# Both late passages with norm, rotation and splits in fixed lanes, key stacks by DMA, and weights rounded by ScalarE outside attention

## The chip, the cores and the metric

The kernel runs on one core of a Trainium2 chip. The core has a matrix engine (TensorE, PE in the profile), three elementwise engines (VectorE is DVE, ScalarE is ACT, GpSimd is POOL) and a queue engine (SyncE, SP) that issues all DMAs of this kernel. Each engine works off its own instructions strictly in order and waits on semaphores for the others. The metric is the time of one execution in microseconds, as the device measures it.

## The reference, cut to what matters

A block of two transformer layers works on 512 latent tokens and, in the first layer, on 256 context tokens, with 1024 channels. Both layers have the same frame:

```python
u_lat = modulate(x_lat, ng[0], ml[0], ml[1])          # rms_norm * g * (1+scale) + shift
...
x_lat = x_lat + ml[2] * rms_norm(y_lat, ng[1])
h_lat = swiglu(modulate(x_lat, ng[2], ml[3], ml[4]), ffn_w_in[l], ffn_w_out[l])
x_lat = x_lat + ml[5] * rms_norm(h_lat, ng[3])
```

The mixer of layer 0 is a gated linear recurrence, that of layer 1 is windowed attention with a sink, 16 query heads on 4 key heads of 64 channels, rotated by position:

```python
q, k, v = jnp.split(u @ w_qkv, [C_Q, C_Q + C_KV], axis=-1)
q = apply_rope(split_heads(q, C_HEADS), cos, sin)
k = apply_rope(split_heads(k, C_KV_HEADS), cos, sin)
k_c, v_c = jnp.split(u_c @ w_qkv[:, C_Q:], 2, axis=-1)
```

So between the FFN of layer 0 and the attention, and again between the attention's output product and the FFN of layer 1, stands the same **passage**: a norm of y over the channels, the residual sum x, a norm of x, and the modulated u, of which the next matrix products are made.

## The kernel before, in words

**Tiles.** Activations lie with channels on the 128 partitions: eight tiles of 128 x 512 for the latents, one for each 128 channels. The latents go through the passages in two halves of 256 tokens, `HS[0]` and `HS[1]`, so that the products of one half can run beside the passage of the other.

**Split products.** Every product is made of three matmuls: an operand is rounded to a high part ("hi", `whi`, `uh`), the rest is the low part ("lo", `wlo`, `ul`), and hi x hi, lo x hi and hi x lo are added in PSUM (`gemm`, L180, and L190 to L192 with the operands swapped). A weight tile of 128 x 1024 floats comes by DMA as `raw` (512 KB, four buffers), hi is made of it by ScalarE (L132, and L154 for weights that are held over) or by GpSimd (L130), lo by VectorE (L133, L155) or GpSimd. Which engine takes the next weight is a pattern per phase, set by `engines(ph)` at L540: 'a' or 'p' for hi, 'd' or 'p' for lo. In before, hi is GpSimd's in all phases that the table doesn't name (the late recurrent phases, the layer-0 output phases, attention), and in every second weight of 'wo'.

**A passage.** `Acc.add` squares a tile on ScalarE (L348, L352) and sums the squares into two accumulators, one kept by VectorE and one by GpSimd (both L353). `rstd_bc` sums over the channels with matmuls against ones (L369), takes the root (L371, ScalarE) and the reciprocal (L373, VectorE), and spreads it over the partitions by matmuls into PSUM (L376); its product `ps_tr` is called bc here. `residual` (L435) then makes x of each tile: in a tile marked 'd', VectorE multiplies y by bc (L451) and adds it, scaled, to x (L454); in a tile marked 'p', VectorE multiplies (L447) and GpSimd adds (L449). `norm_mod` (L393) makes `nt` (L417, VectorE), `uh` (L424, ScalarE) and `ul` (L408, VectorE) of each tile.

**The two late passages.** Passage 1 (`lat_next`, L1311) stands between `po`, the FFN output of layer 0, and the attention's products of keys and values (`kv_ctx`, `kv_lat`) and queries (`q_lat`). Passage 2 (`lat_next2`) stands between `wo`, the attention's output product, and `ffn_in` of layer 1. The generators of a passage and of a product are interleaved by `merge(main, side, ratio)`. Keys are rotated by `roped` (`rx`, `ry`, L1354 to L1358) and stored by `k_stack` twice over the partitions, hi and lo (`KC` for the context, `KL` for the latents): for each key head two copies on ScalarE (L1346, L1347) and two subtractions on VectorE (L1348, L1349), each of 64 partitions.

**Order.** A scheduler with a timeline of its own orders each engine's instructions over the whole program; the kernel is built three times with other buffer slots, and the build whose own simulated time is least is taken. `follow(key, ins)` fixes that instructions with the same key stand on their engine in the order in which they are written ("a lane"). In before, each residual and each norm has a key of its own, for VectorE alone, so the two halves of a passage are free against each other.

## Time and profile before

The profiled execution took 1795.28 us; its span, from the first to the last instruction, is 1793.5 us, so 1.8 us lie around the span. The median of the runs shown is 1795.77 us (1793.75 to 1797.13).

| engine | busy us | share of the span |
|---|---|---|
| PE | 1723.8 | 96% |
| DVE | 1048.4 | 58% |
| ACT | 773.5 | 43% |
| POOL | 386.0 | 22% |

The mean granted clock of PE is 0.981. In the strip of 40 slices (each 44.8 us), the digit is the busy share in tenths:

```profile
PE   7989999999899999999999999799999899999997
DVE  3767644565767636797643536688755853322336
ACT  3965464244645545532222223434756643222311
POOL 1123403343320015200000002424443300000015
PEclk9989999999999999999999999899999999999999
```

PE is full but for the head, the slice from 448 us, those about 1125 to 1215 us (passage 1), about 1390 us (passage 2), and the end. Rows of the timeline read: start, duration, engine, line, operation, out<-in, shape, and in brackets how long the engine was idle before it and what released it.

### The profile page before, as it was taken

The numbers are of one execution on the slowest core, as the hardware profiler recorded it, in microseconds if no ns is written. First come the engines' busy times: TensorE is split into PE (matmuls) and PEld (weight loads), VectorE is DVE, ScalarE is ACT, GpSimd is POOL, SyncE is SP. The second block draws the span as 40 slices with busy tenths as digits, with TensorE's granted clock in tenths as the row PEclk, the third lists the DMA queues.
The fourth block names the chain that finished last, engine by engine and source line by source line (L and its number), as shares of the span: only waits on it lengthen the run. The fifth ranks groups of instructions, "written<-read, shape, count | busy, mean of one in ns | idle before, by whom it ended". The sixth has DMA issues, their size and how long they took to land. (4 is left out here: it accounts for less than half of the span.)

```text
span 1793.5 us, 27238 instructions
## 1 busy us (share of the span) xinstructions
PE 1723.8 (96%) x10711; PEld 1477.9 (82%) x10711; DVE 1048.4 (58%) x1723; ACT 773.5 (43%) x1342; POOL 386.0 (22%) x421
## 2 busy tenths in 40 slices
PE   7989999999899999999999999799999899999997
PEld 3978678798899989988888888787787898888886
DVE  3767644565767636797643536688755853322336
ACT  3965464244645545532222223434756643222311
POOL 1123403343320015200000002424443300000015
PEclk9989999999999999999999999899999999999999
DMA  8546656211345554767545324312021443233323
GB/s 307 162 130 201 205 171 215 69 48 48 92 121 148 170 156 136 240 211 227 174 147 167 119 74 126 95 40 68 2 60 36 130 130 94 83 99 113 94 66 115
DMA packets 83696, 228.18 MB, mean 127 GB/s; under 512 B 9296, under 2 KB 14160, under 8 KB 83568
## 3 DMA queue, kind: packets, MB, share of 16 engines
q1 hardware_dynamic: 83568, 226.45, 41.1%
q8 instruction: 84, 1.38, 0.3%
q14 instruction: 44, 0.36, 0.1%
HBM read 224.31 MB, written 2.10 MB: 126 GB/s over the span
## 5 line engine op out<-in xcount | busy, mean ns | idle before, releaser
L133 DVE TENSOR_TENSOR wlo<-raw,whi 128x1024 fp32r<-128x1024 f32 (+3 forms) x302 | 365.6, 1213 | 298.2 <-ACT whi L132 235.5
L132 ACT CAST whi<-raw 128x1024 fp32r<-128x1024 f32 (+2 forms) x232 | 235.2, 1015 | 478.9 <-issue 176.1
L180 PE MATMUL ps_mm<-uh,whi 128*128 128x256 f32 (+1 forms) x840 | 289.9, 345 | 3.1 <-ACT whi L132 2.9
L180 PE MATMUL ps_mm<-ul,whi 128*128 128x256 f32 (+1 forms) x840 | 287.2, 342 | 0.0
L180 PE MATMUL ps_mm<-uh,wlo 128*128 128x512 f32 (+1 forms) x840 | 286.9, 342 | 0.0
L180 PE MATMUL ps_kv<-uh,whi 128*128 128x512 f32 (+1 forms) x696 | 246.5, 354 | 0.0
L180 PE MATMUL ps_kv<-uh,wlo 128*128 128x512 f32 (+1 forms) x696 | 245.3, 352 | 0.4 <-DVE wlo L133 0.4
L180 PE MATMUL ps_kv<-ul,whi 128*128 128x512 f32 (+1 forms) x696 | 245.4, 353 | 0.0
L130 POOL TENSOR_SCALAR whi<-raw 128x1024 fp32r<-128x1024 f32 (+1 forms) x80 | 79.1, 991 | 727.1 <-PE ps_mm L180 349.3
L180 PEld LDWEIGHTS ps_mm<-uh,whi 128*128 128x128 f32 x840 | 161.8, 193 | 25.1 <-ACT whi L132 3.4
L180 PEld LDWEIGHTS ps_mm<-ul,whi 128*128 128x128 f32 x840 | 161.6, 192 | 17.9 <-issue 1.4
L180 PEld LDWEIGHTS ps_mm<-uh,wlo 128*128 128x128 f32 x840 | 161.4, 192 | 18.1 <-issue 0.6
L180 PEld LDWEIGHTS ps_kv<-uh,whi 128*128 128x128 f32 x696 | 131.8, 189 | 22.4 <-issue 2.7
L353 POOL TENSOR_TENSOR acc<-acc,sq 128x256 f32<-128x256 f32 (+1 forms) x79 | 92.6, 1174 | 261.2 <-ACT sq L352 260.2
L180 PEld LDWEIGHTS ps_kv<-uh,wlo 128*128 128x128 f32 x696 | 131.6, 189 | 18.7 <-DVE wlo L133 0.6
L180 PEld LDWEIGHTS ps_kv<-ul,whi 128*128 128x128 f32 x696 | 131.8, 189 | 17.6
L190 PE MATMUL ps_mm<-whi,uh 128*128 128x256 f32 x344 | 101.5, 296 | 9.2 <-ACT gate L793 9.2
L290 DVE SCALAR_TENSOR_TENSOR aacc<-ar,s,aacc 128x512 f32<-128x512 f32 x112 | 81.7, 755 | 35.3 <-DMA ar<-in_ada_dram 34.5
L180 PE MATMUL ps_kv<-hh,whi 128*128 128x512 f32 (+1 forms) x282 | 100.2, 355 | 0.0
L180 PE MATMUL ps_kv<-hh,wlo 128*128 128x512 f32 (+1 forms) x282 | 100.1, 355 | 0.0
L180 PE MATMUL ps_kv<-hl,whi 128*128 128x512 f32 (+1 forms) x282 | 100.0, 355 | 0.0
L191 PE MATMUL ps_mm<-wlo,uh 128*128 128x256 f32 x344 | 99.2, 290 | 0.0
(325 smaller groups left out, 3493.8 us busy)
## 6 DMA issues: line engine op xcount, KB each, us to landing
raw<-in_ff_in_dram SPq DMA_DIRECT2D x138, 512.0 KB, 3.6
ar<-in_ada_dram SPq DMA_DIRECT2D x192, 256.0 KB, 4.2
raw<-in_ff_out_dram SPq DMA_DIRECT2D x52, 512.0 KB, 3.6
raw<-in_rec_a_dram SPq DMA_DIRECT2D x34, 512.0 KB, 4.3
raw<-in_rec_v_dram SPq DMA_DIRECT2D x16, 512.0 KB, 3.6
raw<-in_rec_g_dram SPq DMA_DIRECT2D x16, 512.0 KB, 4.3
raw<-in_rec_o_dram SPq DMA_DIRECT2D x16, 512.0 KB, 4.0
...
```

What stands on the lines that cost most here:

```text
L130: nc.gpsimd.tensor_scalar(hi[:, :n], raw[:, :n], 1.0, 0.0, ALU.mult, ALU.add)
L132: nc.scalar.copy(hi[:, :n], raw[:, :n])
L133: (nc.gpsimd if cfg["lo"][q % len(cfg["lo"])] == "p" else nc.vector).tensor_sub(lo[:, :n], raw[:, :n], hi[:, :n].bitcast(F32))
L180: mm(ps_, a, b, start=(i == 0), stop=(i == len(q) - 1))
L190: mm(ps, ah, hi[:, s], start=(k == 0), stop=False)
L191: mm(ps, ah, lo[:, s], start=False, stop=False)
L290: nc.vector.scalar_tensor_tensor(a, raw, s_, a, ALU.mult, ALU.add)
L353: (nc.vector if i else nc.gpsimd).tensor_add(d, d, q)
```

## The change

Six edits go together:

1. `engines`: hi by ScalarE in every phase but attention, where it stays with GpSimd; lo by VectorE everywhere.
2. Both passages: all tiles of all halves 'd' (VectorE multiplies and adds), one lane key for residual and norm, "next" for both halves of passage 1, "next2a" and "next2b" for the halves of passage 2; `uh` on ScalarE stands in the lane too. With `own=2` the squares of the last two tiles are not added to an accumulator but summed over directly by more matmuls against ones.
3. The last tile of an output product that runs in halves (`po`, and `pf` of layer 1) keeps its square apart in the same way.
4. `k_stack`: one cast (`kth`, ScalarE) and one subtraction (`ktl`, VectorE, in lane "next") on all 128 partitions, and then eight DMAs from SBUF to SBUF of 64 partitions by SP for each of the six calls. The context's keys are read from PSUM, without the copy `kc`.
5. `q_lat` for the first two query tiles runs by halves: the half `HS[0]` inside passage 1, beside the passage of the other half, and `HS[1]` behind `kv_lat(1)`. Their two weights are loaded and split twice.
6. `behind`: the splits of the weights m >= 1 of layer 1's `ffn_in` stand on their engines behind lane "next2a".

```diff
-        cfg["hi"], cfg["lo"] = {'ra': ['a', 'd'], 'co': ['a', 'ddp'], 'rb': ['a', 'd'], 'ci': ['a', 'd'], 'kv': ['a', 'ddp'], 'wo': ['pa', 'd'], 'l0': ['a', 'd'], 'f1': ['a', 'd'], 'lo2': ['p', 'dp'], 'kw': ['a', 'd']}.get(ph, ("p", "d"))
+        cfg["hi"], cfg["lo"] = ("p" if ph == "at" else "a"), "d"
...
-    def residual(tiles, ys, yacc, gg, j, xacc, sl, pat=""):
+    def residual(tiles, ys, yacc, gg, j, xacc, sl, pat="", key=None, own=0):
...
-                xacc.add(tiles[i][:, :, sl], sl, None, i >= st.ntile - 0)
+                xacc.add(tiles[i][:, :, sl], sl, None, i >= st.ntile - own)
...
-                    yacc.add(y, sl, 0, m >= KD - 0)
+                    yacc.add(y, sl, 0, n == 256 and m >= KD - 1)
...
+            cfg["behind"] = lane_ if m else None
...
+        yield from residual(xl, yl2, yla2, gg2, 0, xla, HS[h], "dddddddd", "next", 2)
+        yield from norm_mod(xl, xla, G1, ada1[0], 0, u3, HS[h], key="next")
...
-            nc.scalar.copy(kh[own], a)
-            nc.scalar.copy(kh[oth], a)
-            nc.vector.tensor_sub(kl[own], a, kh[own].bitcast(F32))
-            nc.vector.tensor_sub(kl[oth], a, kh[own].bitcast(F32))
+        th, tl = ut([P, 512], F32R, name="kth")[:, :n], ut([P, 512], F32R, name="ktl")[:, :n]
+        nc.scalar.copy(th, src)
+        follow("next", nc.vector.tensor_sub(tl, src, th.bitcast(F32)))
+        for i, t in enumerate((th, tl)):
+            for h in range(2):
+                for o in range(2):
+                    nc.sync.dma_start(out=kcols(i, 2 * m + h, c0, n)[64 * o : 64 * o + 64].bitcast(F32),
+                                      in_=t[64 * h : 64 * h + 64].bitcast(F32))
...
-    drain(merge(seq(kv_ctx(), kv_lat(0)) if 1 else seq(kv_lat(0), kv_ctx()), lat_next(1), 2.5))
-    drain(kv_lat(1))
+    drain(merge(seq(kv_ctx(), kv_lat(0), q_lat(QH, HS[0])), lat_next(1), 2.5))
+    drain(kv_lat(1), q_lat(QH, HS[1]))
...
-    drain(q_lat(range(4)))
+    drain(q_lat(range(2, 4)))
...
+        key = "next2" + "ab"[h]
+        yield from residual(xl, yw, ywa, gg1, 0, xla1, HS[h], "dddddddd", key, 2)
+        yield from norm_mod(xl, xla1, G2, ada1[3], 0, u4, HS[h], key=key)
```

The change also moves instructions, since the scheduler orders the whole program anew. Three places follow; numbers at the end of a name are buffer numbers of that build, and line numbers of the changed kernel are some 7 to 11 higher (L447 is then L457, L451 L461, L454 L464, L417 L426, L408 L417, L373 L381, L133 L140, L155 L162).

**VectorE, norm of the first half in passage 1.** In before, behind the fourth `nt`, stand the eight multiplications of the second half's residual (y with bc 11024; the second to the eighth are shown) and four splits of the context's keys (KC), ahead of the third `ul`:

```order
L447 SCALAR_TENSOR_TENSOR y_7932<-y_7932,gv_3219,ps_tr_11024 128x256
L447 SCALAR_TENSOR_TENSOR y_7933<-y_7933,gv_3219,ps_tr_11024 128x256
L447 SCALAR_TENSOR_TENSOR y_7934<-y_7934,gv_3219,ps_tr_11024 128x256
L447 SCALAR_TENSOR_TENSOR y_7935<-y_7935,gv_3219,ps_tr_11024 128x256
L447 SCALAR_TENSOR_TENSOR y_7936<-y_7936,gv_3219,ps_tr_11024 128x256
L447 SCALAR_TENSOR_TENSOR y_7937<-y_7937,gv_3219,ps_tr_11024 128x256
L447 SCALAR_TENSOR_TENSOR y_7938<-y_7938,gv_3219,ps_tr_11024 128x256
L1348 TENSOR_TENSOR KC_10969<-kc_11007,KC_10967 64x256
L1349 TENSOR_TENSOR KC_10969<-kc_11007,KC_10967 64x256
L1348 TENSOR_TENSOR KC_10969<-kc_11007,KC_10967 64x256
L1349 TENSOR_TENSOR KC_10969<-kc_11007,KC_10967 64x256
L408 SCALAR_TENSOR_TENSOR ul_10789<-nt_10938,ada_8071,uh_10781 128x256
```

Now (bc of the norm is 10930, that of the second half 11030) the norm's tiles stand together to the eighth `ul`, and the key split and the second half's residual come behind it:

```order
L417 SCALAR_TENSOR_TENSOR ul_10790<-nt_10948,ada_8071,uh_10782 128x256
L426 SCALAR_TENSOR_TENSOR nt_10956<-xl_7162,gv_10325,ps_tr_10930 128x256
L417 SCALAR_TENSOR_TENSOR ul_10791<-nt_10952,ada_8071,uh_10783 128x256
L426 SCALAR_TENSOR_TENSOR nt_10960<-xl_7164,gv_10325,ps_tr_10930 128x256
L417 SCALAR_TENSOR_TENSOR ul_10792<-nt_10956,ada_8071,uh_10784 128x256
L417 SCALAR_TENSOR_TENSOR ul_10793<-nt_10960,ada_8071,uh_10785 128x256
L1354 TENSOR_TENSOR ktl_11010<-ps_mm_10984,kth_11009 128x256
L461 TENSOR_TENSOR y_7931<-y_7931,ps_tr_11030 128x256
L464 SCALAR_TENSOR_TENSOR xl_7150<-y_7931,gv_3219,xl_7150 128x256
L1354 TENSOR_TENSOR ktl_11062<-ps_mm_11036,kth_11061 128x256
```

What moved: the second half's residual and the key splits stand behind the whole norm of the first half, the adds of GpSimd are gone, and four splits of 64 partitions have become one of 128.

**VectorE, norm of the first half in passage 2.** In before, behind the reciprocal stand two low parts of streamed `ffn_in` weights (wlo 14236 and 14287) and two halves of a held one (kwl), ahead of and between the first tiles:

```order
L373 RECIPROCAL rs_13832<-sd_13830 128x2
L133 TENSOR_TENSOR wlo_14236<-raw_14233,whi_14235 128x1024
L417 SCALAR_TENSOR_TENSOR nt_13872<-xl_7150,gv_12587,ps_tr_13834 128x256
L417 SCALAR_TENSOR_TENSOR nt_13875<-xl_7152,gv_12587,ps_tr_13834 128x256
L133 TENSOR_TENSOR wlo_14287<-raw_14284,whi_14286 128x1024
L155 TENSOR_TENSOR kwl_14186<-raw_14183,kwh_14185 128x512
L155 TENSOR_TENSOR kwl_14190<-raw_14183,kwh_14189 128x512
L408 SCALAR_TENSOR_TENSOR ul_13817<-nt_13872,ada_9022,uh_13809 128x256
L417 SCALAR_TENSOR_TENSOR nt_13914<-xl_7154,gv_12587,ps_tr_13834 128x256
L408 SCALAR_TENSOR_TENSOR ul_13818<-nt_13875,ada_9022,uh_13810 128x256
```

Now the held halves stand ahead of the reciprocal, and the norm follows it at once:

```order
L162 TENSOR_TENSOR kwl_14203<-raw_14200,kwh_14202 128x512
L162 TENSOR_TENSOR kwl_14207<-raw_14200,kwh_14206 128x512
L381 RECIPROCAL rs_13942<-sd_13940 128x2
L426 SCALAR_TENSOR_TENSOR nt_13982<-xl_7150,gv_12695,ps_tr_13944 128x256
L426 SCALAR_TENSOR_TENSOR nt_13985<-xl_7152,gv_12695,ps_tr_13944 128x256
L417 SCALAR_TENSOR_TENSOR ul_13923<-nt_13982,ada_9022,uh_13915 128x256
L426 SCALAR_TENSOR_TENSOR nt_14024<-xl_7154,gv_12695,ps_tr_13944 128x256
L417 SCALAR_TENSOR_TENSOR ul_13924<-nt_13985,ada_9022,uh_13916 128x256
L426 SCALAR_TENSOR_TENSOR nt_14028<-xl_7156,gv_12695,ps_tr_13944 128x256
L417 SCALAR_TENSOR_TENSOR ul_13925<-nt_14024,ada_9022,uh_13917 128x256
```

What moved: no split of a streamed weight is left between the reciprocal and the norm's tiles.

**SP, behind the passage.** In before the last loads of query weights (`raw_..<-in_qk_w_dram`) stand close together, with the rotation tables and the mask between them:

```order
L124 DMA raw_11880<-in_qk_w_dram 128x1024
L124 DMA raw_12008<-in_qk_w_dram 128x1024
L1324 DMA rope_10963<-in_rope_dram 128x512
L1324 DMA rope_10964<-in_rope_dram 128x512
L1414 DMA atm_sb<-in_atm_dram 128x1152
L124 DMA raw_12153<-in_qk_w_dram 128x1024
L144 DMA raw_12695<-in_wo_w_dram 128x1024
L144 DMA raw_12818<-in_wo_w_dram 128x1024
L124 DMA raw_12959<-in_wo_w_dram 128x1024
```

Now (the first row is the last key copy of the first half, atm_sb the mask, KL_10973 to KL_10980 the second half):

```order
L1358 DMA KL_10980<-ktl_11254 64x256 x2
L1422 DMA atm_sb<-in_atm_dram 128x1152
L1358 DMA KL_10973<-kth_11459 64x256 x2
L1358 DMA KL_10974<-kth_11459 64x256 x2
L1358 DMA KL_10977<-ktl_11460 64x256 x2
L1358 DMA KL_10978<-ktl_11460 64x256 x2
L1358 DMA KL_10975<-kth_11502 64x256 x2
L1358 DMA KL_10976<-kth_11502 64x256 x2
L1358 DMA KL_10979<-ktl_11503 64x256 x2
L1358 DMA KL_10980<-ktl_11503 64x256 x2
L131 DMA raw_12261<-in_qk_w_dram 128x1024
L151 DMA raw_12803<-in_wo_w_dram 128x1024
```

What moved: the key copies ("x2" is two of the same row, 48 in all) stand between the mask and the last loads, and each holds the queue until the part of the keys that it copies is made.

More of the change, by code (lines that the diff above doesn't have):

```diff
@@ L129, in wload @@
             if cfg["hi"][q % len(cfg["hi"])] == "p":
-                nc.gpsimd.tensor_scalar(hi[:, :n], raw[:, :n], 1.0, 0.0, ALU.mult, ALU.add)
+                behind(nc.gpsimd.tensor_scalar(hi[:, :n], raw[:, :n], 1.0, 0.0, ALU.mult, ALU.add))
             else:
-                nc.scalar.copy(hi[:, :n], raw[:, :n])
-            (nc.gpsimd if cfg["lo"][q % len(cfg["lo"])] == "p" else nc.vector).tensor_sub(
-                lo[:, :n], raw[:, :n], hi[:, :n].bitcast(F32))
+                behind(nc.scalar.copy(hi[:, :n], raw[:, :n]))
+            behind((nc.gpsimd if cfg["lo"][q % len(cfg["lo"])] == "p" else nc.vector).tensor_sub(
+                lo[:, :n], raw[:, :n], hi[:, :n].bitcast(F32)))
         return hi, lo
@@ L151, in whold @@
                 if cfg["hi"][q % len(cfg["hi"])] == "p":
-                    nc.gpsimd.tensor_scalar(hi, raw[:, c], 1.0, 0.0, ALU.mult, ALU.add)
+                    behind(nc.gpsimd.tensor_scalar(hi, raw[:, c], 1.0, 0.0, ALU.mult, ALU.add))
                 else:
-                    nc.scalar.copy(hi, raw[:, c])
-                (nc.gpsimd if cfg["lo"][q % len(cfg["lo"])] == "p" else nc.vector).tensor_sub(lo, raw[:, c], hi.bitcast(F32))
+                    behind(nc.scalar.copy(hi, raw[:, c]))
+                behind((nc.gpsimd if cfg["lo"][q % len(cfg["lo"])] == "p" else nc.vector).tensor_sub(
+                    lo, raw[:, c], hi.bitcast(F32)))
                 out_.append((hi, lo))
@@ L391, in sumsq, with norm_mod @@
         return a
-    def norm_mod(tiles, acc, G, sh, j, u, sl, st=None):
+    def norm_mod(tiles, acc, G, sh, j, u, sl, st=None, key=None):
         if acc is not None:
@@ L399, in norm_mod @@
         late = []
-        key = uid("nm") if 1 else None
+        lane_a = key is not None
+        key = key or uid("nm")
         def low(i, t):
@@ L423, in norm_mod @@
                     follow(key, nc.vector.tensor_scalar(t[:, r, :], t[:, r, :], g_, None, ALU.mult))
-                nc.scalar.activation(u[0][i][:, r, sl], t[:, r, :], AF.Identity, bias=sh[:, j, k : k + 1])
+                follow(key if lane_a else None,
+                       nc.scalar.activation(u[0][i][:, r, sl], t[:, r, :], AF.Identity, bias=sh[:, j, k : k + 1]))
             if acc is None and 0:
@@ L1353, in roped @@
         x = ut([P, 512], name="rx")[:, :n]
-        nc.vector.stream_shuffle(x, p_, swap)
+        key = "next" if n == 256 else None
+        follow(key, nc.vector.stream_shuffle(x, p_, swap))
         y = ut([P, 512], name="ry")[:, :n]
-        nc.vector.tensor_mul(y, p_, cosT[:, sl])
+        follow(key, nc.vector.tensor_mul(y, p_, cosT[:, sl]))
         nc.gpsimd.tensor_mul(x, x, sinT[:, sl])
-        nc.vector.tensor_add(y, y, x)
+        follow(key, nc.vector.tensor_add(y, y, x))
         return y
@@ L1376, in kv_ctx @@
             p_ = qk_proj(8 + m, uc3, SC, FC)
-            kc = ut([P, 256], name="kc")
-            nc.scalar.copy(kc, p_)
-            k_stack(kc, m, 0, 256)
+            k_stack(p_, m, 0, 256)
             yield
@@ L1556, in block_kernel @@
     kf = [(m, q) for m in range(2) for q in range(2)]
-    drain(merge(seq(ffn_in(SL, 1, u4, hl1, range(N0), HS[0], 0, hold_f, kf),
-                    ffn_in(SL, 1, u4, hl1, range(N0), HS[1], 0, hold_f, kf)), lat_next2(1), 2.2))
+    drain(merge(seq(ffn_in(SL, 1, u4, hl1, range(N0), HS[0], 0, hold_f, kf, "next2a"),
+                    ffn_in(SL, 1, u4, hl1, range(N0), HS[1], 0, hold_f, kf, "next2a")), lat_next2(1), 2.2))
+    cfg["behind"] = None
     yf, yfa = new_ys(SL), Acc(SL, DY)
```

33 lines of the change are left out of this document (14 added, 19 removed).

## The prediction

> **What bounds the kernel now.** I read the page first: PE is busy in 96% of the span, so the question is only where the other 4%, and the time at a low clock, lie. The table of windows by stage tells it (start and end; length; busy us of PE, PEld, DVE, ACT, POOL with counts; PE's clock; DMA share; GB/s):
>
> ```profile
> 430.00:470.00 40.00, 29.86 (x217) 27.55 (x216) 31.87 (x43) 29.63 (x47) 17.04 (x25) 0.89 0.16 45
> 470.00:1125.00 655.00, 652.16 (x3921) 576.21 (x3920) 395.19 (x554) 251.47 (x394) 84.29 (x65) 1.00 0.51 157
> 1125.00:1215.00 90.00, 78.59 (x496) 73.25 (x496) 68.19 (x140) 36.53 (x83) 32.60 (x35) 0.91 0.20 63
> 1215.00:1385.00 170.00, 163.03 (x1138) 124.14 (x1137) 114.15 (x352) 101.38 (x247) 74.22 (x88) 0.99 0.14 41
> 1385.00:1417.00 32.00, 26.52 (x191) 25.33 (x190) 27.34 (x45) 20.15 (x46) 14.21 (x13) 0.89 0.48 146
> ```
>
> PE stands still 10.1 us before 470, 11.4 in passage 1 (90 - 78.59), 7.0 in attention and 5.5 in passage 2, and in both passages its clock is down. Between 470 and 1125 it is full, with ACT idle most of the time. The view of waits then names what PE waited for, the first three lines in 1125 to 1215, the last in 1380 to 1420:
>
> ```profile
> PE ps_kv L180 <- DVE ul L408: 5.1, 1, 5.1
> PE ps_tr L369 <- POOL acc L353: 2.6, 1, 2.6
> PE ps_kv L180 <- ACT uh L424: 2.2, 1, 2.2
> ...
> PE ps_mm L180 <- ACT uh L424: 4.3, 1, 4.3
> ```
>
> Windows of 5 us show what follows a wait of 2.6 us or more, PE full and slow, and that PE fed by a busy DVE need not be slow (1175):
>
> ```profile
> 1130.00:1135.00 5.00, 4.52 (x21) 4.52 (x22) 0.22 (x2) 1.13 (x2) 1.11 (x2) 0.51 0.64 210
> 1135.00:1140.00 5.00, 5.00 (x37) 5.00 (x37) 4.00 (x7) 1.91 (x5) 3.44 (x2) 0.80 0.44 112
> 1175.00:1180.00 5.00, 4.55 (x32) 4.27 (x33) 4.82 (x13) 3.35 (x7) 0.00 (x0) 1.00 0.00 0
> ...
> 1380.00:1385.00 5.00, 4.11 (x33) 2.69 (x30) 1.40 (x4) 2.49 (x5) 0.00 (x0) 1.00 0.00 0
> ...
> 1410.00:1415.00 5.00, 4.29 (x16) 3.71 (x17) 5.00 (x11) 3.94 (x10) 0.92 (x1) 0.50 0.84 261
> 1415.00:1420.00 5.00, 5.00 (x38) 5.00 (x36) 3.26 (x8) 2.18 (x5) 0.00 (x0) 0.81 0.60 182
> ```
>
> One such stretch costs about 3 us: in the first two rows 4.52 x 0.49 + 5 x 0.20 = 3.2, in the last two 4.29 x 0.50 + 5 x 0.19 = 3.1.
>
> **Passage 1, before.** The chain of waits and the timelines of PE, DVE and POOL give its steps:
>
> ```profile
> 1130.48 1.02 PE L369 MATMUL ps_tr<-ones,acc 128*128 128x1 f32 x4 [2.62 <-POOL acc L353]
> 1137.43 0.42 DVE L451 TENSOR_TENSOR y<-y,ps_tr 128x256 f32<-128x256 f32 x1 [0.93 <-PE ps_tr L376]
> 1139.84 0.41 DVE L451 TENSOR_TENSOR y<-y,ps_tr 128x256 f32<-128x256 f32 x1
> 1140.29 0.48 DVE L454 SCALAR_TENSOR_TENSOR xl<-y,gv,xl 128x256 f32<-128x256 f32 x1
> ...
> 1137.39 4.67 PE ps_mm L180 x39
> 1147.82 0.80 PE ps_tr L369 x8
> 1150.05 0.87 DVE L417 SCALAR_TENSOR_TENSOR nt<-xl,gv,ps_tr 128x256 f32<-128x256 f32 x2 [0.94 <-PE ps_tr L376]
> 1152.75 3.22 DVE L447 SCALAR_TENSOR_TENSOR y<-y,gv,ps_tr 128x256 f32<-128x256 f32 x8
> 1153.31 6.26 POOL L449 TENSOR_TENSOR xl<-xl,y 128x256 f32<-128x256 f32 x8 [6.33 <-DVE y L447]
> 1159.01 0.84 DVE L408 SCALAR_TENSOR_TENSOR ul<-nt,ada,uh 128x256 fp32r<-128x256 f32 x1
> 1159.90 0.58 PE L180 MATMUL ps_kv<-ul,kwh 128*128 128x256 f32 x1 [5.14 <-DVE ul L408]
> 1163.89 0.47 DVE L417 SCALAR_TENSOR_TENSOR nt<-xl,gv,ps_tr 128x256 f32<-128x256 f32 x1
> 1164.28 0.48 DVE L408 SCALAR_TENSOR_TENSOR ul<-nt,ada,uh 128x256 fp32r<-128x256 f32 x1
> 1188.62 4.12 PE ps_kv L180 x18
> ```
>
> PE stood still from 1127.86 (1130.48 - 2.62), with 12 matmuls of the last `po` block done since the block of the tile before; a matmul of 256 columns takes 4.67 / 39 = 0.12 us, so that earlier block ended at 1126.4. The queries q0 to q3 begin at 1188.62: 96 matmuls of 512 columns at 4.12 / 18 = 0.229 end at about 1210.5. So the stretch takes 84 us. The 5.1 us of waiting for `ul` is a matter of order: the norm of the first half is interrupted by eight multiplications of the second half and by key splits, from 1152.75 to 1159.01, with POOL adding beside them.
>
> **Passage 1, after.** I replay the new order with these durations, from the same 1126.4.
>
> 1. The last `po` tile's square is no longer added, so the sums over the channels wait only for the add of the tile before, and stand ahead of most of the last block. No row shows when that add ends now; between no wait and the 2.6 above I take 1.2, near the middle because one of the two adds is gone. With the sums 0.5, the 24 remaining matmuls 2.9 and bc 0.7: 1131.7 instead of 1137.4.
> 2. The residual is eight tiles of about 0.85 (L451 0.41 and L454 0.48, which overlap a little), two weight splits of 1.2 (row 1406.42 below) and two sums of 0.5 like an L454 that stand between: 10.2. PE has 96 matmuls of the context's keys and values, 11.5 us, which cover it: the sums follow at 1143.3.
> 3. From sums to the first `nt` it took 1150.05 - 1147.82 = 2.2: 1145.5. The norm's 16 instructions at 0.39 (1163.89 to 1164.28) run through: 6.3, and 0.5 for the last matmuls: 1152.3. PE is paced here.
> 4. 112 matmuls of the first half (second key tile, values, q0 and q1 but for eight): 13.4, and bc of the second half 0.7: 1166.4. The second half's residual, some 8 us on DVE, lies beside them.
> 5. First `uh` of the second half 1.0; then 72 matmuls (8.6) beside the norm, a rotation, its split and one weight split on DVE, 8.9 together: 1176.3.
> 6. Values' rest, q0 and q1 of the second half, 72 matmuls: 8.6, 1184.9. Then q2 and q3, 48 of 512 columns, 11.0: 1195.9.
>
> That is 14.6 us earlier than 1210.5; the halving of q0 and q1 (96 x 0.12 against 48 x 0.229, +0.5) is in it. I take off 2 for one stretch at half clock behind the idle and paced time of steps 2 to 3, which is likelier than not: **-12.5**, with bounds of -16 (no wait in step 1, no such stretch) and -8 (two stretches of 3 and a slower step 5).
>
> The Trainium skill, "TensorE: Matmul & The Clock Gate", Part 1, says that the clock is halved after an idle window of about 3.4 us and that this window runs freely. Idle time of 2.6 us was enough here; by the rule, luck of the phase decides, and the sum would be -14.5 without a halving and -11.5 with a full one.
>
> **The key stacks.** The copies now cost SP and DMA, for which the nearest rows are a weight load's issue and the rotation tables' landing:
>
> ```profile
>   L144 SPq DMA_DIRECT2D raw<-in_ff_in_dram x3: 327/327/328, 1393.4 to 1399.2; - x3
> ...
> rope<-in_rope_dram SPq DMA_DIRECT2D x2, 256.0 KB, 2.7
> ```
>
> 48 issues of 0.33 us are 15.8 us of SP. The last 16 stand behind the second half's rotation, at about 1180, and their four last issues and landing end some 4 us later, 12 us ahead of the first scores. The loads of query weights behind them are for tiles q4 and later, which the attention uses. So nothing: 0; if that cover failed, the first scores would wait at most the 16 issues and the landing, 5.3 + 2.7 = 8. A copy between two places on the chip is in no row; below zero it can't go beyond what step 5 already counts.
>
> **Passage 2.**
>
> ```profile
> 1401.91 0.15 DVE L373 RECIPROCAL rs<-sd 128x2 f32<-128x2 f32 x1
> 1406.42 1.23 DVE L133 TENSOR_TENSOR wlo<-raw,whi 128x1024 fp32r<-128x1024 f32 x1 [4.36 <-ACT whi L132]
> 1407.57 0.86 DVE L417 SCALAR_TENSOR_TENSOR nt<-xl,gv,ps_tr 128x256 f32<-128x256 f32 x2
> ...
> 1405.34 1.05 ACT L132 CAST whi<-raw 128x1024 fp32r<-128x1024 f32 x1 [6.19 <-DMA raw<-in_ff_in_dram]
> ...
> 1402.21 0.68 PE L376 MATMUL ps_tr<-ident,rs 128*128 128x128 f32 x4 [0.38 <-DVE rs L373]
> ```
>
> `nt` was ready at 1402.9, when bc was done, and began at 1407.57, because a weight split whose data had not landed stood ahead of it. The stretch lost 5.5 of idle time, 3.1 of clock and 0.9 just before 1385, 9.5 in all. Now the norm stands right behind the reciprocal. What stays: PE waits 0.4 for the reciprocal and 1.5 for the first `uh`, and since the splits for m >= 1 now stand behind the norm, about 1.0 for the first of them. **-6.5**; the bounds are -3 (one stretch at half clock stays) and -9.
>
> **The weights.** GpSimd rounded 80 of them; the windows are of L130 alone:
>
> ```profile
> L130 POOL TENSOR_SCALAR whi<-raw 128x1024 fp32r<-128x1024 f32 (+1 forms) x80 | 79.1, 991 | 727.1 <-PE ps_mm L180 349.3
> ...
> 110.00:430.00 320.00, 35.58 (x30) 0.98 0.47 146
> 430.00:470.00 40.00, 4.02 (x3) 0.89 0.16 45
> ...
> L190 PE MATMUL ps_mm<-whi,uh 128*128 128x256 f32 x344 | 101.5, 296 | 9.2 <-ACT gate L793 9.2
> ```
>
> Nearly all go to ACT at 1.05 each (the cast at 1405.34). Where PE is full and ACT idle (470 to 1125, 251 of 655) they cost nothing. Where PE waits for ACT it counts: in 430 to 470 it waits 9.2 us for the copies `gate`, behind tables and exponentials, and in the new order four more casts stand there. At worst all delay the chain, +4.2, and others 2; at best the order of that stage falls out better, -2; half of the casts: **+2**. Attention, whose rounding stays and whose idle 7.0 is of many small waits, I cost 0, between -3 and +3. At the very end the last square's add goes, but bc of the half before it comes 10 matmuls (1.2 us) later: 0, within 0.6 either way.
>
> **Sum.** 1795.28 - 12.5 - 6.5 + 2 = 1778.3, rounded 1778. The profiled execution is 0.5 below the median of the runs, so the same holds for the median.
>
> **Rivals.**
>
> - *ACT becomes the bound before 470 and the kernel is slower.* 33 of the 80 casts lie between 110 and 470. If each stands ahead of a copy or exponential that PE waits for, that is 33 x 1.05 = 35 us, and 1795.28 - 19 + 35 = 1811. It decides from the point where more than about 22 of them are on the path (19 + 3.6 us of 1.05). For it: the waits for `gate`. Against it: before 430 PE is full most of the time, and only four new casts stand in the stage that waits.
> - *The lanes pace PE instead of freeing it.* All adds are now DVE's, and a clock once low may stay low while DVE feeds PE. Then passage 1 gives 8, passage 2 gives 3 and the early stages take 4: 1788. For it: steps 3 and 5. Against it: from 1175 to 1180 a DVE at 4.82 of 5 fed PE at full clock.
> - *The key copies come late.* The Trainium skill, "DMA: Bandwidth & Descriptors", "Rules for kernel authors", advises against many small transfers: under 64 KB they are mostly overhead, and these are of 64 KB. As a mechanism here it is the 8 us above, in front of the first scores: 1786. No run shows such a copy yet; the 12 us of cover speak against it.
> - *The new order only moves the waits.* The whole program is ordered anew, and what the passages win comes back in the head, the gate stage and attention, each at its worst bound (6 + 3, and passage 1 at -8, passage 2 at -3): 1793 to 1795, no change.
>
> **How the numbers follow.** A measurement of this kernel can tell about 0.2%, 3.6 us, from no change. Forecast 0.60, own range 1768 to 1786; pacing 0.15; late copies 0.04; no change 0.10; slower 0.11. The range runs from 1766 (bounds: -16, -9, -2, -3 give 1765) to 1797, which leaves out the slower case and a little below. Faster 0.79, same 0.10, slower 0.11.
>
> **What would show it.** Right: between the last `po` block and the first scores some 70 us instead of 84, `nt` to the eighth `ul` of the first half in one piece of 6 to 7 us, no idle time over 2.5 us on PE in 1125 to 1200; in passage 2 `nt` within 1.2 us of the reciprocal and a clock of 1.00. Wrong: waits for KC or KL copies in front of scores; clock 0.5 in the passages; more than 12 us of waiting for `gate` before 470; PE waiting for weights of `ffn_in` behind the norm.

## The result, and the profile after

| | before | after |
|---|---|---|
| median of the runs, us | 1796.05 (1793.75 to 1797.13) | 1783.33 (1783.1 to 1786.01) |
| profiled execution, us | 1795.28 | 1783.1 |
| its span, us | 1793.5 | 1780.7 |
| its mean clock of PE | 0.981 | 0.986 |
| busy us PE, DVE, ACT, POOL | 1723.8, 1048.4, 773.5, 386.0 | 1723.4, 1037.3, 828.4, 279.4 |

The ratio is 0.9937, with an interval from 0.9925 to 0.9949. The forecast was 1778. PE has the same busy time; ACT has 55 us more and POOL 107 less, from the casts and the adds.

Three events cut both executions into stretches. The first is the start of the last `po` block, which is the last FFN tile of the second half, at its first matmul with a weight `whi`. The second is the first score, and the third the last `ps_o` product of the attention. Rows of the timeline, and of the views of one tile (last two times: first and last start), of before and then of after give them:

```profile
1126.26 0.28 PE L180 MATMUL ps_kv<-hh,whi 128*128 128x256 f32 x1
L1446 PE MATMUL ps_kv<-KC,QS x64: 277/283/582, 1208.9 to 1360.9; 128*128 128x256 f32 x64
L1487 PE MATMUL ps_o<-pT,VT x288: 379/379/431, 1234.5 to 1382.6; 128*64 128x256 f32 x144
```

```profile
1119.65 0.36 PE L188 MATMUL ps_kv<-hh,whi 128*128 128x256 f32 x1
L1454 PE MATMUL ps_kv<-KC,QS x64: 276/355/562, 1197.0 to 1355.0; 128*128 128x256 f32 x64
L1495 PE MATMUL ps_o<-pT,VT x288: 379/379/689, 1225.6 to 1374.7; 128*64 128x256 f32 x144
```

The windows from the first of these times on, of before and of after (length, busy us of PE, PEld, DVE, ACT, POOL, PE's clock, DMA share, GB/s):

```profile
1126.30:1208.90 82.60, 71.19 (x453) 66.65 (x453) 62.08 (x127) 34.18 (x79) 29.49 (x33) 0.90 0.19 58
1208.90:1382.60 173.70, 167.62 (x1159) 128.29 (x1159) 118.45 (x360) 101.35 (x246) 77.01 (x90) 0.99 0.15 43
1382.60:1793.50 410.90, 392.86 (x2117) 341.60 (x2113) 179.84 (x257) 128.27 (x207) 52.41 (x58) 0.98 0.34 101
```

```profile
1119.70:1197.00 77.30, 73.32 (x522) 69.98 (x523) 56.74 (x131) 28.76 (x63) 13.32 (x16) 0.93 0.37 108
1197.00:1374.70 177.70, 169.62 (x1159) 128.74 (x1160) 122.25 (x359) 104.03 (x248) 75.36 (x88) 0.98 0.14 42
1374.70:1780.70 406.00, 393.27 (x2141) 342.22 (x2137) 174.26 (x261) 142.61 (x230) 28.45 (x25) 0.99 0.33 102
```

The span is 12.8 us shorter: 6.6 come from ahead of passage 1, 5.3 from passage 1, 4.9 from behind the attention, and the attention gave back 4.0. The prediction had put 12.5 in passage 1, 6.5 in passage 2, and a loss of 2 ahead. The sum came out 5 us short of the forecast, its terms further off: an error of 7.2 in passage 1 and one of 8.6 ahead of it nearly cancel, which is luck.

The windows of after that answer to those of the prediction, and PE's longest wait of after between 1115 and 1215:

```profile
430.00:470.00 40.00, 33.84 (x276) 31.99 (x276) 34.44 (x43) 36.29 (x56) 13.63 (x23) 1.00 0.19 59
1125.00:1215.00 90.00, 86.02 (x569) 80.12 (x568) 70.92 (x160) 32.77 (x72) 18.81 (x20) 0.94 0.35 101
1385.00:1417.00 32.00, 32.00 (x268) 31.78 (x267) 27.02 (x52) 22.37 (x47) 8.50 (x8) 1.00 0.51 166
```

```profile
PE ps_mm L188 <- DVE ul L417: 2.6, 1, 2.6
...
```

Passage 2 runs full at full clock. Passage 1 has idle time of 4.0 us (90 - 86.02) where it had 11.4, but its clock is only 0.94, against 0.91 in before.

### The profile page after: what moved, and what is told of

The parts are those of the page before. It is cut to its first block, busy times and chain, and to the rows that moved or that the text cites. A ratio compares the mean times of both kernels' runs of the same rounds, so it can differ in the third digit from the quotient of the medians.

```text
span 1780.7 us, 27528 instructions
## 1 busy us (share of the span) xinstructions
PE 1723.4 (97%) x10807; PEld 1478.9 (83%) x10807; DVE 1037.3 (58%) x1741; ACT 828.4 (47%) x1403; POOL 279.4 (16%) x316
## 4 chain that ended last, share of the span: by engine, by line
PE 88%; DVE 5%; ACT 4%; issue 2%; DMA 0%; SPq 0%; POOL 0%; DVEq 0%; ACTq 0%
PE ps_mm L188 35%; PE ps_kv L188 31%; PE ps_o L1495 2%; PE ps_o L231 2%; PE ps_tr L1488 2%; PE ps_mm L198 2%; PE ps_mm L199 2%; PE ps_mm L200 2%; PE ps_mm L266 1%; PE ps_kv L266 1%; PE ps_tr L231 1%; PE ps_kv L1454 1%; PE ps_tr L377 1%; PE ps_kv L231 1%; ACT whi L139 1%
## 5 line engine op out<-in xcount | busy, mean ns | idle before, releaser
L139 ACT CAST whi<-raw 128x1024 fp32r<-128x1024 f32 (+3 forms) x304 | 298.2, 982 | 568.5 <-issue 215.6
L140 DVE TENSOR_TENSOR wlo<-raw,whi 128x1024 fp32r<-128x1024 f32 (+3 forms) x314 | 365.9, 1166 | 332.8 <-ACT whi L139 322.7
L188 PE MATMUL ps_mm<-uh,whi 128*128 128x512 f32 (+1 forms) x808 | 277.0, 343 | 2.9 <-ACT whi L139 2.9
L188 PE MATMUL ps_mm<-ul,whi 128*128 128x512 f32 (+1 forms) x808 | 274.7, 340 | 0.0
L188 PE MATMUL ps_kv<-uh,whi 128*128 128x512 f32 (+1 forms) x744 | 260.6, 350 | 0.0
L188 PE MATMUL ps_kv<-uh,wlo 128*128 128x512 f32 (+1 forms) x744 | 259.5, 349 | 0.4 <-DVE wlo L140 0.4
L188 PE MATMUL ps_kv<-ul,whi 128*128 128x512 f32 (+1 forms) x744 | 259.7, 349 | 0.0
L188 PE MATMUL ps_mm<-hh,wlo 128*128 128x256 f32 (+1 forms) x299 | 99.8, 334 | 0.9 <-DVE wlo L140 0.9
L188 PE MATMUL ps_mm<-hh,whi 128*128 128x256 f32 (+1 forms) x299 | 100.0, 334 | 0.0
L188 PE MATMUL ps_mm<-hl,whi 128*128 128x256 f32 (+1 forms) x299 | 99.6, 333 | 0.0
L200 PE MATMUL ps_mm<-whi,ul 128*128 128x256 f32 x344 | 98.7, 288 | 0.0
```

The costliest lines, as they stand in the source:

```text
L139: behind(nc.scalar.copy(hi[:, :n], raw[:, :n]))
L140: behind((nc.gpsimd if cfg["lo"][q % len(cfg["lo"])] == "p" else nc.vector).tensor_sub(lo[:, :n], raw[:, :n], hi[:, :n].bitcast(F32)))
L188: mm(ps_, a, b, start=(i == 0), stop=(i == len(q) - 1))
L200: mm(ps, al, hi[:, s], start=False, stop=(k == KD - 1))
```

## The experiments

The kernels are taken from three builds with other buffer slots each, and before runs its first build, the changed kernel its third. Up to the first place that an edit touches, kernels of the same build with the same engine table have the same order; of the experiments all but e2 are third builds. The ratio is taken against before as it ran beside that kernel, where before's median was between 1793.58 and 1796.05, so ratios and not medians compare kernels of different rows. The stretches of each profiled execution are cut by the same events (us; "rest" runs from the last `ps_o` to the end of the span):

| kernel | median (range) | ratio (interval) | ahead | passage 1 | attention | rest |
|---|---|---|---|---|---|---|
| before | 1796.05 (1793.75 to 1797.13) | 1 | 1126.3 | 82.6 | 173.7 | 410.9 |
| after | 1783.33 (1783.1 to 1786.01) | 0.9937 (0.9925 to 0.9949) | 1119.7 | 77.3 | 177.7 | 406.0 |
| e1 before, third build | 1808.04 (1806.41 to 1809.73) | 1.0076 (1.0061 to 1.0091) | 1132.2 | 78.3 | 182.5 | 411.6 |
| e2 after, first build | 1783.18 (1781.39 to 1788.76) | 0.9943 (0.9925 to 0.9961) | 1127.7 | 78.3 | 174.7 | 406.3 |
| e3 rounding only | 1789.91 (1786.49 to 1791.53) | 0.9975 (0.9964 to 0.9986) | 1122.4 | 76.5 | 178.4 | 408.8 |
| e5 rounding, passage 2 | 1784.09 (1782.36 to 1789.19) | 0.9937 (0.992 to 0.9953) | 1124.0 | 77.1 | 181.3 | 405.0 |
| e6 rounding, lanes of passage 1 | 1798.16 (1793.21 to 1802.28) | 1.0014 (1.0001 to 1.0027) | 1122.8 | 83.1 | 180.7 | 410.4 |
| e7 after, old key stacks | 1788.32 (1786.05 to 1789.17) | 0.9962 (0.9947 to 0.9976) | 1123.9 | 77.4 | 179.9 | 405.9 |
| e8 after, queries whole | 1787.48 (1781.79 to 1788.47) | 0.9952 (0.9933 to 0.9971) | 1119.0 | 76.8 | 178.2 | 406.0 |
| e4 after, keys out of the lane | 1782.31 (1780.99 to 1784.15) | 0.9934 (0.9919 to 0.9948) | 1120.3 | 78.7 | 173.6 | 405.9 |
| e9 after, squares added | 1778.75 (1778.5 to 1778.95) | 0.9913 (0.9894 to 0.9932) | 1119.4 | 74.6 | 177.2 | 405.9 |
| e11 e9, keys free, last tile | 1778.93 (1776.22 to 1780.05) | 0.9913 (0.9898 to 0.9928) | 1123.4 | 74.7 | 173.9 | 405.1 |
| e12 all VectorE, no lane | 1776.03 (1775.65 to 1777.7) | 0.9893 (0.9876 to 0.9909) | 1123.3 | 73.3 | 174.1 | 405.2 |
| e10 after, no lanes in passage 1 | 1772.43 (1771.96 to 1775.39) | 0.9882 (0.9865 to 0.9899) | 1119.1 | 71.9 | 173.6 | 405.9 |

A stretch is one profiled execution. How far chance moves one is seen in the column "ahead": the eleven third builds with the new engine table have the same order there, and yet six lie at 1122.4 to 1124.0 and five, after among them, at 1119.0 to 1120.3. The last section shows the event that parts them.

### The builds and the rounding

**e1_before_third** takes before's third build, **e2_after_first** the changed kernel's first:

```diff
-    for _ in range(3):
+    for i_ in range(3):
...
-        if best is None or (ns < best[1] if "min" == "min" else True):
+        if i_ == 2:
```

> The kernel before, but the third of its three builds (other buffer slots) instead of the one that its own timeline takes, the first. The changed kernel runs its third build. Theory A, the 6.7 us by which the changed kernel reaches passage 1 earlier come from the other slots: passage 1 starts (end of the po block of the tile before the last, first half) near 1120 us and the time is near 1789. Theory B, they come from the rounding on ScalarE: it starts near 1126 and the time stays near 1796.

> The changed kernel, but its first build. Theory A (slots): passage 1 starts near 1126 instead of 1119.7, time near 1790. Theory B (rounding): it starts near 1120, time near 1783.

Neither theory holds for e1: the third build of before is 0.76% slower than its first, so a third build is not by itself what makes the changed kernel faster. The changed kernel is as fast from either build, though in e2's profile, its slowest execution (1788.76), passage 1 begins at 1127.7. But the other build alone moves passage 1 from 82.6 to 78.3 with no other edit.

**e3_rounding_only** is before with the new engine table, which also gives all low parts to VectorE:

```diff
-        cfg["hi"], cfg["lo"] = {'ra': ['a', 'd'], ...}.get(ph, ("p", "d"))
+        cfg["hi"], cfg["lo"] = ("p" if ph == "at" else "a"), "d"
```

> The kernel before with the new table of rounding alone; its order up to passage 1 is that of the changed kernel. Theory, the passages are worth what the traces show (passage 1 6.6 and passage 2 5.8 less 5.4 given back in attention, tail 0.9 worse): the time is 1783.3 + 6.1 = about 1789.5, with 84 us from the start of passage 1 to the end of q3. Rival, nearly all of the gain is from ahead of passage 1: about 1785.

Rounding on ScalarE is a gain of 0.25%, and against e1, of the same build, of 18 us. The time is that of the theory, but not for its reason: passage 1 takes 76.5 and not 84, with nothing else changed, and what e3 lacks against after lies elsewhere. The stretch ahead is 1122.4. Waits of e3 in 1115 to 1215 (compare the first lines with those of before in the prediction) and its window of passage 1:

```profile
PE ps_kv L180 <- DVE ul L408: 5.2, 1, 5.2
...
PE ps_tr L369 <- POOL acc L353: 0.3, 1, 0.3
```

```profile
1122.40:1198.90 76.50, 68.03 (x453) 63.30 (x452) 61.76 (x127) 32.81 (x77) 22.76 (x27) 0.96 0.16 52
```

The wait for `ul`, which the lanes were to remove, stands as before at 5.2. What went is the wait for the sum of squares (2.6, now 0.3) and the half clock behind it (0.90, now 0.96).

### The two passages apart

**e5_rounding_p2** adds to e3 the lanes, own squares and `behind` of passage 2:

```diff
+        key = "next2" + "ab"[h]
+        yield from residual(xl, yw, ywa, gg1, 0, xla1, HS[h], "dddddddd", key, 2)
...
+    drain(merge(seq(ffn_in(SL, 1, u4, hl1, range(N0), HS[0], 0, hold_f, kf, "next2a"),
```

> Rounding by ScalarE and the new passage 2 (lanes, all tiles on VectorE, squares kept apart, the splits behind the norm), passage 1 and the keys as before; third build, so that the order up to passage 2 is that of e3_rounding_only. Theory, passage 2 is worth what e3 and the changed kernel show between the last product of attention and the end of PE, 395.4 against 391.8: time 1786. Rival, the 6.5 of the prediction: 1783.

The median lies between theory and rival, and the ratio is that of the whole change, 0.9937: so passage 1, key stacks and halved queries together bring nothing to the time. The rest takes 405.0 against 408.8 in e3.

**e6_rounding_lanes1** adds to e3 the lanes, VectorE's adds and the own squares of passage 1, with the old key stacks and whole queries:

```diff
+        yield from residual(xl, yl2, yla2, gg2, 0, xla, HS[h], "dddddddd", "next", 2)
+        yield from norm_mod(xl, xla, G1, ada1[0], 0, u3, HS[h], key="next")
```

> Rounding by ScalarE and the lanes of passage 1 (all tiles on VectorE, two squares kept apart), but key stacks, queries and passage 2 as before; third build. In e3 PE waits 5.2 us for a ul that stands behind the second half's multiplications, and then runs at half clock. Theory, the lane takes both away: the stretch from passage 1 to the end of q3 falls from 76.7 to 69 to 72 and the time to 1783 to 1786. Rival, the wait only moves to the second half, whose residual now comes later: 75 to 78, time 1788 to 1791.

The rival had the mechanism, and neither had the size: lanes, adds and own squares together cost 6.6 us in the passage (83.1 against 76.5). The timeline of PE shows two of the waits, both in front of the sums of the second half:

```profile
1161.22 0.58 PE L377 MATMUL ps_tr<-ones,acc 128*128 128x1 f32 x2 [4.33 <-POOL acc L361]
1164.87 0.59 PE L377 MATMUL ps_tr<-ones,acc 128*128 128x1 f32 x2 [3.07 <-DVE acc L361]
```

In a lane the second half's residual may begin only when the whole norm of the first half is through. It begins at 1152.15, with rotations and old key splits between its tiles, and ends at 1165.2; PE has run out of work for the first half at 1156.9.

### Parts taken out of the change

**e7_old_key_stacks** puts back the old `k_stack`, **e8_queries_whole** the old queries:

```diff
-        th, tl = ut([P, 512], F32R, name="kth")[:, :n], ut([P, 512], F32R, name="ktl")[:, :n]
...
+            nc.scalar.copy(kh[own], a)
+            nc.scalar.copy(kh[oth], a)
+            nc.vector.tensor_sub(kl[own], a, kh[own].bitcast(F32))
+            nc.vector.tensor_sub(kl[oth], a, kh[own].bitcast(F32))
```

```diff
-    drain(merge(seq(kv_ctx(), kv_lat(0), q_lat(QH, HS[0])), lat_next(1), 2.5))
-    drain(kv_lat(1), q_lat(QH, HS[1]))
+    drain(merge(seq(kv_ctx(), kv_lat(0)), lat_next(1), 2.5))
+    drain(kv_lat(1))
```

> The changed kernel with the key stacks of before (copies and subtractions of 64 partitions by ScalarE and VectorE, no DMAs). Theory, the DMAs take 32 of 48 instructions from two engines that pace PE there: with the old ones the stretch is 2 to 4 us longer, 79.5 to 81.5, time 1785 to 1787. Rival, the copies by DMA only hold SP and the tiles they read, and are worth nothing: 77.5, time 1783.

> The changed kernel with q0 to q3 in whole tiles behind the passage, as before; third build. Theory, the halves give PE work beside the second half's passage: without them the stretch is 4 to 6 us longer, 81 to 83, time 1787 to 1789. Rival, the halves only add matmuls and VectorE work: 76 to 78, time 1782 to 1784.

The passage takes 77.4 and 76.8 without the one or the other, as both rivals had it: neither edit alone is worth anything beside the lane. e6 (83.1) lacks both, and besides the own square of `po`, the lane for the rotation and the new passage 2: with these and any one of the two edits, what e6 lost in the passage is covered. Which of them does it was not tried apart. The higher medians come from other stretches: e7's from ahead, where its order is that of after, and the attention; three runs of e8 are some 6 above its profiled one, at a mean clock of 0.982 to 0.984 instead of 0.986. They are not put down to the edits.

**e4_keys_free** takes the rotation and the key split out of the lane, and **e9_squares_added** the own squares of passage 1's residual:

```diff
-        follow("next", nc.vector.tensor_sub(tl, src, th.bitcast(F32)))
+        nc.vector.tensor_sub(tl, src, th.bitcast(F32))
...
-        key = "next" if n == 256 else None
+        key = None
```

```diff
-        yield from residual(xl, yl2, yla2, gg2, 0, xla, HS[h], "dddddddd", "next", 2)
+        yield from residual(xl, yl2, yla2, gg2, 0, xla, HS[h], "dddddddd", "next", 0)
```

> The changed kernel with rotation and key split taken out of the lane of passage 1 (all else in it). Theory, the rotation of the second key tile with its waits for GpSimd and ScalarE, fixed ahead of the second half's norm, costs PE 2.6 us and a stretch at half clock: without it the stretch to the end of q3 is 3 to 5 us shorter, 72 to 75 instead of 77.5, and the time 1779 to 1781. Rival, VectorE is simply full there: no change, 1783.

> The changed kernel, but in passage 1 all squares of x are added to the two accumulators (own 0 instead of 2); third build. The changed kernel shows 46 records of matmuls against ones there instead of 24, 6.6 us instead of 4.1. Theory, these sums are on PE's path: without them the stretch from passage 1 to the end of q3 is 1 to 2 us shorter, 75.5 to 76.5, time 1781 to 1782.5. Rival, PE would wait for the adds instead, as e6 did by 7.4 us: 79 to 85, time 1785 to 1791.

Freeing the keys only moved the waits (2.1 for the second half's reciprocal and 2.6 for its first `uh` in place of the 2.6 for `ul`), and the passage took 78.7: the theory fails. Adding the squares again won 2.7 there (74.6), more than the theory's 1 to 2; the ratio falls from 0.9937 to 0.9913, with intervals that overlap a little. The windows of the sums against ones alone, 1118 to 1200, of after and of e9:

```profile
1118.00:1200.00 82.00, 6.41 (x48) 6.65 (x48) 0.94 0.38 111
```

```profile
1118.00:1200.00 82.00, 3.91 (x32) 4.09 (x32) 0.96 0.39 111
```

16 records less are 2.5 us of busy PE. Ends of matmuls are modelled; from each start to PE's next start, with waits left out, the timelines give 5.6 and 3.4 us, so 2.2. The records are of one column each and take PE 0.10 to 0.13 us (3.4 / 32 to 6.41 / 48), nearly as long as a matmul of 256 columns (0.12). To sum squares by PE is no saving where PE is the bound.

**e10_no_lanes1** keeps the rounding, the DMA stacks, the halves and passage 2, and gives passage 1's residual and norm their old engines and free order, with all squares of x added and rotation and key split out of the lane as well:

```diff
-        yield from residual(xl, yl2, yla2, gg2, 0, xla, HS[h], "dddddddd", "next", 2)
-        yield from norm_mod(xl, xla, G1, ada1[0], 0, u3, HS[h], key="next")
+        yield from residual(xl, yl2, yla2, gg2, 0, xla, HS[h], {'ln1': 'pppppppp', ..., 'ln0': 'dddpdddp', ...}.get("ln%d" % h, ""))
+        yield from norm_mod(xl, xla, G1, ada1[0], 0, u3, HS[h])
```

> The changed kernel with passage 1 in the patterns of before, without lanes and with all squares added, but with the key stacks by DMA, the halves of q0 and q1, and the new passage 2; third build. Theory, with PE work of its own beside the passage and fewer splits on VectorE, the lanes and the full VectorE patterns matter little: 75 to 79, time 1781 to 1785. Rival, without a lane the first half's norm is interrupted again, as in e3 (wait of 5.2 us and a stretch at half clock): 82 to 86, time 1788 to 1792.

It is the fastest of all, better than theory and rival: 1.18% below before, where the changed kernel has 0.63%, and the intervals are apart. Of the 10.2 us between the two spans 5.4 lie in passage 1 and 4.1 in the attention, which has the same instructions. e5 differs from e10 only in the old key stacks, whole queries and the added squares of `po` and `pf`, and has 77.1 in the passage and 0.9937: so these edits are worth something without the lanes (0.55%), and nothing with them (after against e5). Its window of passage 1, its PE waits in 1115 to 1215, and two rows of its DVE timeline:

```profile
1119.10:1191.00 71.90, 68.91 (x507) 66.48 (x507) 56.94 (x124) 29.07 (x65) 22.42 (x28) 0.95 0.41 118
```

```profile
PE ps_mm L188 <- ACT uh L434: 1.4, 1, 1.4
...
PE ps_mm L188 <- DVE ul L417: 0.3, 1, 0.3
```

```profile
1141.79 2.83 DVE L457 SCALAR_TENSOR_TENSOR y<-y,gv,ps_tr 128x256 f32<-128x256 f32 x7 [0.23 <-PE ps_tr L384]
...
1160.19 0.86 DVE L426 SCALAR_TENSOR_TENSOR nt<-xl,gv,ps_tr 128x256 f32<-128x256 f32 x2
```

Seven multiplications of the second half still stand inside the norm of the first, as in before, and yet PE no longer waits 5 us for `ul`: the norm of the first half takes longer than in after (13.9 us instead of 7.8), but the second half's first `nt` starts at 1160.19, 41.1 after the stretch began, against 43.2 in after (1162.89 - 1119.65).

**e11_mixed** (squares added, keys free, last tile of `pf` added as in before) and **e12_vector_no_lane** (e10 with all adds on VectorE, and the same last tile) ask whether the engine or the lane costs:

```diff
-                    yacc.add(y, sl, 0, n == 256 and m >= KD - 1)
+                    yacc.add(y, sl, 0, n == 256 and m >= KD - 1 and l == 0)
...
-        yield from residual(xl, yl2, yla2, gg2, 0, xla, HS[h], {'ln1': 'pppppppp', ...}.get("ln%d" % h, ""))
+        yield from residual(xl, yl2, yla2, gg2, 0, xla, HS[h], "dddddddd")
```

> Meant as a better version: the changed kernel with all squares of x added in passage 1, rotation and key split out of the lane, and the last product's last square added as before; third build. If the sums (1 to 2 us), the lane of the rotation (1 us in e4) and the end (0.9 us: 14.1 instead of 13.2 from the last product to the end of the span) each count by themselves: 1779 to 1781. Rival, each takes the place of a wait that then appears: 1783 to 1787.

> e10 with all tiles of passage 1 on VectorE ('d', as in the changed kernel) but without lanes, and the last product's last square added as before (that shows at the end alone: 13.3 instead of 14.1 us there); third build. e10 and e9 differ in lanes and in who adds; this run parts them. Theory, the lane is what costs: 71 to 73 from passage 1 to the end of q3, as in e10 (72.1), time 1770.5 to 1773. Rival, what helps in e10 is GpSimd, which makes the second half's sums beside VectorE: 75 to 78, time 1775 to 1779.

With all adds on VectorE and no lane the passage takes 73.3, just above the theory's 73, with a time in the rival's range; with the lane (e11, whose time is near that of its theory) 74.7, with GpSimd's adds (e10) 71.9. The windows of e11 and e12:

```profile
1123.40:1198.10 74.70, 69.45 (x508) 66.77 (x507) 57.75 (x134) 29.53 (x65) 17.77 (x18) 0.95 0.40 114
1123.30:1196.60 73.30, 68.95 (x507) 66.60 (x507) 57.98 (x134) 29.60 (x65) 15.55 (x18) 0.95 0.39 113
```

So by these profiles lane and engine are worth 1.4 each, and the own squares 2.7: together the 5.4 from after to e10. Part of that is the clock, whose low stretches take 5.1 from after's passage (73.32 x 0.07) and 3.4 from e10's (68.91 x 0.05). Each figure is one profiled execution, and the intervals of e11, e12 and e10 overlap from one to the next. Clear of noise are after against e10 and e12, whose intervals are apart, and e9 and e11 against e10, which ran beside them and whose ranges are apart. What the lane alone costs (e11 against e12) stays open between nothing and a few us.

## Why the prediction came out as it did

**Passage 1 (predicted -12.5, measured -5.3).** The forecast's direction held, its size did not. Idle time went from 11.4 (82.60 - 71.19) to 4.0 (77.30 - 73.32). The rows of its steps, of PE and DVE in after, against the replay moved to the start at 1119.65:

```profile
1123.64 0.60 PE L384 MATMUL ps_tr<-ident,rs 128*128 128x128 f32 x4
...
1138.81 0.87 DVE L426 SCALAR_TENSOR_TENSOR nt<-xl,gv,ps_tr 128x256 f32<-128x256 f32 x2 [0.87 <-PE ps_tr L384]
...
1140.00:1145.00 5.00, 4.50 (x20) 4.18 (x21) 4.37 (x12) 3.80 (x10) 0.00 (x0) 0.50 0.12 32
...
1146.09 0.48 DVE L417 SCALAR_TENSOR_TENSOR ul<-nt,ada,uh 128x256 fp32r<-128x256 f32 x1 [0.18 <-ACT uh L434]
...
1162.25 0.60 PE L384 MATMUL ps_tr<-ident,rs 128*128 128x128 f32 x4
...
1186.13 0.40 PE L188 MATMUL ps_mm<-uh,whi 128*128 128x512 f32 x1
```

- Step 1 (bc 5.3 after the start) was right in time: 4.6. Its reason, the square that is no longer added, is not borne out: in e3, which adds it, the wait is 0.3. It goes with the rounding and the new order that comes with it.
- Steps 2 and 3 were right: the first `nt` at 1138.81, where the replay says 1138.75. The norm ran in one piece to the eighth `ul`, 7.8 us with its end at 1146.57 instead of 6.3. Beside it PE ran at half clock: the stretch of low clock for which 2 were taken off.
- Steps 2 to 4 together, from bc to bc of the second half, took 38.6 (1124.24 to 1162.85) and not 34.7. The low clock is some 3.0 of it (4.36 x 0.12 + 4.50 x 0.50 + 4.95 x 0.06 in the three windows of 5 us from 1135 to 1150, of which the middle one is shown). For the rest, the replay forgot that own squares mean 48 sums against ones instead of 24, 6.4 us of busy PE instead of 3.4 in before, 40 of the 48 in these steps.
- **Step 5 is the one that failed**: 9.9 forecast. The queries q2 begin at 1186.13, 72 matmuls (8.6) behind it, so step 5 took from 1162.85 to 1177.5, 14.7. The DVE and PE timelines of after:

```profile
1162.89 0.87 DVE L426 SCALAR_TENSOR_TENSOR nt<-xl,gv,ps_tr 128x256 f32<-128x256 f32 x2 [0.17 <-DMA KL<-ktl]
1163.95 0.48 DVE L417 SCALAR_TENSOR_TENSOR ul<-nt,ada,uh 128x256 fp32r<-128x256 f32 x1 [0.18 <-ACT uh L434]
1164.36 0.46 DVE L1365 STREAM_SHUFFLE rx<-ps_mm 128x256 f32<-128x256 f32 x1
...
1165.03 1.68 DVE L140 TENSOR_TENSOR wlo<-raw,whi 128x1024 fp32r<-128x1024 f32 x1
...
1167.57 0.42 DVE L1354 TENSOR_TENSOR ktl<-ry,kth 128x256 fp32r<-128x256 f32 x1 [0.53 <-ACT kth L1353]
1167.91 0.47 DVE L426 SCALAR_TENSOR_TENSOR nt<-xl,gv,ps_tr 128x256 f32<-128x256 f32 x1
...
1168.84 0.39 PE L188 MATMUL ps_mm<-ul,kwh 128*128 128x256 f32 x1 [2.57 <-DVE ul L417]
...
1170.00:1175.00 5.00, 5.00 (x33) 5.00 (x33) 4.13 (x12) 2.03 (x4) 0.74 (x1) 0.71 0.39 100
```

The prediction added up the durations on DVE (8.9) and set them beside 72 matmuls. But the lane puts the rotation of a key of the first half and its split right behind the first tiles of the norm, with a weight split between them, and the third `nt` waits behind all of it: 4.0 us from 1163.95 to 1167.91. PE has work for two tiles, stands 2.57, and is slow behind it (0.71, which costs 5.00 x 0.29 = 1.5): 4.0 of the 4.8 by which step 5 is too long. The new order removed the interruption that the profile of before shows and had a second of the same kind behind it. The sum of durations on an engine was about right; that PE can use a tile only when it comes was left out. In e4, with rotation and split out of the lane, this wait is gone, but others stand in its place and the passage is no faster (78.7).

The total: -0.7 in step 1, +3.9 in steps 2 to 4, +4.8 in step 5 are 8.0 above the replay's 69.5, of which the prediction had taken 2 for the clock; and its start for before (84) was 1.4 above the 82.6 that the scores show.

So the mechanism of passage 1 was wrong, and not only its size: the lanes with their adds and own squares bring between nothing (with their companions, after against e5) and a loss (e6 against e3, after against e10). The 5.3 us stand in e3 too, without a lane, and most of them in e1, with no edit but the build.

**The weights (predicted +2, measured -6.6 ahead of passage 1).** The sign was wrong. The stage with `gate` fell from 10.1 of idle time at 0.89 to 6.2 at full clock. The waits for `gate` in the two profiles (before's row stands in the prediction):

```profile
L198 PE MATMUL ps_mm<-whi,uh 128*128 128x256 f32 x344 | 100.1, 293 | 4.0 <-ACT gate L804 4.0
L199 PE MATMUL ps_mm<-wlo,uh 128*128 128x256 f32 x344 | 98.8, 288 | 5.1 <-DVE wlo L140 5.1
```

The wait went from 9.2 to 4.0, and a new one for low parts took its place in part. The prediction counted more work for ACT and nothing for the work that leaves GpSimd and the places that the other instructions take then. How this stage comes out hangs on the build as well (e1 and e2 each have 9.2 and 9.7 us of idle time in it, after 6.2), and part of the 6.6 is chance: the third builds with the new table, in the same order, begin passage 1 between 2.3 and 7.3 us earlier than before. So the 6.6 can't be given to one cause; that the rounding is a gain at all is shown by e3 alone, 0.25% against before and more against e1.

**Passage 2 (predicted -6.5, rest of the span -4.9).** Right in its mechanism. Idle time of 5.5 and the low clock are gone (the row 1385 to 1417). With the end's loss of 0.9 set apart, it is -5.8; e5 gives -3.8 of it against e3, smaller than forecast and inside the bounds, and the other 2 came with the rounding. One sign was wrong:

```profile
1393.00 0.16 DVE L381 RECIPROCAL rs<-sd 128x2 f32<-128x2 f32 x1
1396.09 0.87 DVE L426 SCALAR_TENSOR_TENSOR nt<-xl,gv,ps_tr 128x256 f32<-128x256 f32 x2 [2.93 <-PE ps_tr L384]
```

`nt` comes 3.1 behind the reciprocal and not 1.2, since bc is queued on a PE that is busy with other work. It costs nothing there.

**The key stacks (0) and the attention (0 +- 3).** No score waited for a copy, though the cover was thinner than forecast: SP took 0.59 and not 0.33 for an issue, and the last one stands at 1191.6, 5.4 before the first scores (1197.0); the view of DMAs has 2.0 us from issue to landing:

```profile
L1358 SPq DMA_DIRECT2D KL<-ktl x16: 540/594/1366, 1159.6 to 1191.6; - x16
```

The attention took 4.0 longer, just outside the bound. Between kernels whose attention has the same instructions it takes from 173.6 to 182.5, with and without the change's parts (before's third build has the longest), so it is a matter of the order that the scheduler finds, and not assigned to an edit here.

**The end (0, within 0.6).** It lost 0.9: from the last output matmul's start to the end of the span it is 14.2 (1766.53 to 1780.7) instead of 13.2 (1780.27 to 1793.5). The last sums wait for a square whose tile stands on DVE behind the residual of the other half:

```profile
1768.67 0.38 PE L377 MATMUL ps_tr<-ones,sq 128*128 128x1 f32 x2 [1.75 <-ACT sq L342]
```

In before these sums waited 1.89 for GpSimd's add. With the last tile of `pf` added as in before (e11, e12) the same stretch is 13.3.

**The rivals.** ACT as the bound and a slower kernel fell with e3, late key copies since no score waited for one, and no change with the interval of the ratio. That the lanes pace PE came nearest in passage 1 (8 forecast there, 5.3 measured), but the early stages, which that rival had at a loss, hid it in the sum.
